# A two-layer hybrid encoder on one core: a table of offsets to the list scheduler's turns

## The chip, the cores and the metric

The kernel runs on one core of a Trainium2 chip. The time is device microseconds (us) of one execution, median of several runs. The profile is one further execution, read with its own time.

## What is computed

Two encoder layers on x (512 tokens, 1024 features, float32). Per layer, shortened from the reference:

```python
h = rmsnorm(x, norm_mix[i])
qa, ka, va, qb, kb, vb, cq, ckv, kr = jnp.split(h @ w_in[i], split_at, axis=-1)
o_a = dilated_attention(rmsnorm(qa), rmsnorm(ka), va, table_a)     # A: 6 heads, whole rows of 512 keys here
o_b = banded_attention(rmsnorm(qb), rmsnorm(kb), vb, 128, bias_b)  # B: 4 heads, +-128 keys, with a sink
o_c = latent_attention(qc, kc, vc)                                 # C: 6 heads, low rank q and kv, rotary part
mixed = concat(rmsnorm(o_a), rmsnorm(o_b), rmsnorm(o_c))
x = x + mixed @ w_out[i]
h = rmsnorm(x, norm_mlp[i])
x = x + square(relu(h @ w_up[i])) @ w_down[i]
```

## The kernel before

Nothing is issued as it is written. `tile_hybrid_encoder_kernel` calls stand-ins of the engines; each call is recorded (`record`, L171) as an `Op` with its number `i` in program order, its modelled cost on each engine that may run it, and the earlier ops that it needs. At the end `schedule` (L207) lists them: at each turn it takes, of all ops whose needs are met and whose buffers can be had, the one that can start first by the model, and of equal ones the one with the lowest number (L251). An op that either ScalarE or VectorE may run (a copy out of PSUM, the high half of a split) goes where `finish` (L225) has it end sooner, and there too the ops with a lower number count as standing ahead. `emit` (L285) then issues the list, so that every engine and the DMA queue of SyncE run in exactly that order and wait by semaphores. All instructions therefore carry line L295.

The work of a layer, in program order: `win0`, `win(1)`, `win(2)` and the steps w3 to w7 (L911) are slices of the input projection; C0 to C2, A0 to A2, B0 and B1 are pairs of heads; `group` normalises a head group; then the output projection over three groups of columns (L928), and the MLP in four chunks (L969). All products are in float32r from a high and a low half (`mm3`, L403): the names `whi` and `wlo` are the halves of a weight tile of 1024 columns, split from `raw`, of which there are two buffers; four of each half are held. `fm` holds halves of activations.

A head (`attend`, L735) goes in halves of two query blocks. For each block TensorE makes scores (`bank<-qk`), VectorE adds the bias and finds the row's extreme (`p<-bank,ma` and `nm`), ScalarE takes the exponential (`p<-p,nm`), TensorE transposes it in four pieces (`bank<-con_sb,p`), ScalarE and VectorE split that into halves (`pt`), and TensorE multiplies by the values (`bank<-pt,v`, for B `bank<-pt,vb`). Between these the only other work for TensorE is projections (`bank<-whi,fm` and `bank<-wlo,fm`).

Queries and keys of A and B must be laid out twice (`pair_t`, L793): from a transposed tile SyncE's queue copies halves of partitions (`qk<-qk`), six for keys, three for queries, some of which wait for others to land. In the same queue stand the weights, the bias rows (`ma<-brow`) and, for the output projection, the tiles of x (`x_tiles`, L341, loaded at L925): three of the four lie in the buffer `v` of A's values, so that their loads cannot start before A's last product has read it. The projection's result is added to x on VectorE (`v<-bank,grc,v`, L936).

Of the kernel before, what the change touches and what calls it, by code (L numbers as in the profile page):

```python
# [2 lines left out]

# [14 lines left out]
D = 1024  # L18
S = 512
# [9 lines left out]

G1, G2, GO, GQL, GKL, GQA, GKA, GQB, GKB, GQC, GKC, GQR, GKR, SNK, NPAR = (  # L30
    0, 8, 16, 24, 26, 27, 28, 29, 30, 31, 32, 33, 65, 97, 101)


def _head(x, n):
# [11 lines left out]
class View:  # L46


    def __init__(self, buf, a, ops, dtype):
        self.buf, self.a, self.ops, self.dtype = buf, a, ops, dtype  # L50
# [65 lines left out]


class Op:
    __slots__ = ("i", "eng", "name", "args", "kw", "alts", "cost", "after", "need", "todo", "at", "bufs", "end", "start")


class Plan:
# [5 lines left out]

    def __init__(self, tc, pools):
        self.tc, self.pools, self.ops, self.order, self.gate = tc, pools, [], {}, None  # L130

    def tile(self, pool, shape, dtype, tag, name, bufs):
        b = Buf(pool, tuple(shape), dtype, tag, name, bufs, pool == "psum")
        self.order.setdefault(tag, []).append(b)
        return b
# [35 lines left out]
    def record(self, eng, method, args, kw, alt=None):  # L171
        out = kw.get("out", args[0] if args else None)
        outs = [v for v in (out, kw.get("accum_out")) if isinstance(v, View)]
        ins = [v for v in list(args) + list(kw.values()) if isinstance(v, View) and all(v is not w for w in outs)]
        cost = self.cost(eng, method, outs[0] if outs else ins[0], ins)
        if kw.get("accum_out") is not None and eng == "scalar":
            cost += 93.0
        if alt:
            alt.alts[eng] = (method, args, kw, cost)
            return  # L180
        o = Op()
        o.i, o.alts = len(self.ops), {eng: (method, args, kw, cost)}
        o.after, o.need, o.bufs = set(), {self.gate} if self.gate else set(), []
        for views, write in ((ins, False), (outs, True)):
            for v in views:
                b, box = v.buf, v.box()
                if b not in o.bufs:
                    o.bufs.append(b)
                    b.left += 1
                keep = []  # L190
                for e in b.log:
                    bx, op, wr = e
                    hit = bx[0] < box[1] and box[0] < bx[1] and bx[2] < box[3] and box[2] < bx[3]
                    if hit and (write or wr) and op is not o:
                        o.need.add(op)
                    inside = box[0] <= bx[0] and bx[1] <= box[1] and box[2] <= bx[2] and bx[3] <= box[3]
                    if not (write and inside and op is not o):
                        keep.append(e)
                keep.append((box, o, write))
                b.log = keep  # L200
        for p in o.need:
            p.after.add(o)
        o.todo, o.at, o.end = len(o.need), 0.0, None
        self.ops.append(o)
        return o

    def schedule(self):  # L207
        self.order = {t: [b for b in bs if b.left] for t, bs in self.order.items()}
        free = {t: [0.0] * bs[0].bufs for t, bs in self.order.items()}
        head = {t: 0 for t in self.order}  # L210
        placed = set()
        ready = {}
        clock = {}
        for o in self.ops:
            for e in o.alts:
                clock[e] = 0.0
                if not o.todo:
                    ready.setdefault(e, []).append(o)
        result = []
        while len(result) < len(self.ops):  # L220
            best = None
            queue = {e: [(o.i, o.alts[e][3]) for o in c if len(o.alts) == 1 and o.at <= clock[e] + 500.0]
                     for e, c in ready.items()}

            def finish(o, e):  # L225

                wait = 0.25 * sum(x for i, x in queue[e] if i < o.i)
                return max(clock[e], o.at) + wait + o.alts[e][3] + self.LATER.get(e, 0.0)

            for e, c in ready.items():  # L230
                for o in c:
                    if len(o.alts) > 1 and min(o.alts, key=lambda x: finish(o, x)) != e:
                        continue
                    at = max(o.at, clock[e])
                    for b in o.bufs:
                        if b in placed:
                            continue
                        f = free[b.tag]
                        seq = self.order[b.tag]
                        while seq and head[b.tag] < len(seq) and seq[head[b.tag]] in placed:  # L240
                            head[b.tag] += 1
                        skip = 0
                        for x in seq[head[b.tag]:] if b.tag not in self.ANY_ORDER else ():
                            if x is b:
                                break
                            skip += x not in placed
                        if skip >= len(f):
                            at = None
                            break
                        at = max(at, sorted(f)[skip])  # L250
                    if at is not None and (best is None or (at, o.i) < best[:2]):  # L251
                        best = (at, o.i, o, e)
            if best is None:
                raise RuntimeError("no instruction can be issued")
            at, _, o, e = best
            o.eng = e
            o.name, o.args, o.kw, o.cost = o.alts[e]
            o.start, o.end = at, at + o.cost
            clock[e] = o.end
            for a in o.alts:  # L260
                ready[a].remove(o)
            for b in o.bufs:
                if b in placed:
                    continue
                f = free[b.tag]
                f.sort()
                f.pop(max(n for n, x in enumerate(f) if x <= at))
                placed.add(b)
            result.append(o)
            lat = self.LAT[e]  # L270
            for b in o.bufs:
                b.left -= 1
                b.end = max(b.end, o.end + lat)
                if not b.left:
                    free[b.tag].append(b.end)
            for d in o.after:
                d.todo -= 1
                to_pe = "tensor" in d.alts
                d.at = max(d.at, o.end + (0.0 if e == "tensor" and to_pe else lat + (130.0 if to_pe else 0.0)))
                if not d.todo:  # L280
                    for a in d.alts:
                        ready.setdefault(a, []).append(d)
        return result
# [871 lines left out]
```

## Time and profile before

| | |
|---|---|
| time, median of 3 runs | 1229.56 us (1227.28 to 1229.75) |
| the profiled execution: its own time | 1230.45 us |
| its span, first to last instruction | 1228.7 us |
| TensorE matmul busy | 1203.5 us, 98%, 6624 instructions |
| TensorE weight loads busy | 1032.6 us, 84% |
| VectorE busy | 1014.5 us, 83% |
| ScalarE busy | 629.0 us, 51% |
| DMA, mean share of 16 engines | 31.7% for the queue of SyncE |
| mean granted TensorE clock | 0.993 |

1.75 us of the profiled time lie around the span. A matmul's record is longer than the interval to the next one, since they overlap in the array; so a busy share of 98% says that TensorE seldom stood quite empty, and not that it was fed as fast as it can go. The interval between starts tells the rate. The granted clock is a share of 2.4 GHz: 1.00 is 2.4 GHz, 0.50 is 1.2 GHz.

### The profile page before, as it was taken

How to read it: one execution, taken by the hardware profiler on the slowest of the kernel's cores; microseconds unless marked ns; L12 is line 12 of the kernel's file. 1: busy time of each engine (PE TensorE's matmuls, PEld its weight loads, DVE VectorE, ACT ScalarE, POOL GpSimd, SP SyncE). 2: the span in 40 equal slices, each digit the busy share in tenths (PEclk: the TensorE clock that was granted, in tenths of full speed). 3: DMA queues.
4: the chain of work that ended last, by engine and by line, in shares of the span. 5: the costliest groups of instructions: out<-in, count | busy, mean ns of one | idle time of the engine just before them, and what ended most of it. 6: DMA issues, size and time to landing. Idle time of an engine off the chain costs nothing.

```text
span 1228.7 us, 17782 instructions
## 1 busy us (share of the span) xinstructions
PE 1203.5 (98%) x6624; PEld 1032.6 (84%) x6624; DVE 1014.5 (83%) x1907; ACT 629.0 (51%) x1232; POOL 3.5 (0%) x10
## 2 busy tenths in 40 slices
PE   9999999899999999999999999898999999999998
PEld 8998979788888888888899989786888888888886
DVE  7799879798796886977958996997978869779686
ACT  6658678455343333333546684965544334334342
POOL 1000000000000000000000000000000000000000
PEclk9999999899999999999999999998999999999999
DMA  6311254533133042140152114454331422422301
GB/s 197 125 52 53 50 147 132 150 137 121 68 122 118 35 173 102 71 135 20 53 166 72 50 52 102 136 146 136 131 117 38 165 79 79 155 71 103 103 1 69
DMA packets 36357, 123.89 MB, mean 101 GB/s; under 512 B 4700, under 2 KB 5852, under 8 KB 32176
## 3 DMA queue, kind: packets, MB, share of 16 engines
q1 hardware_dynamic: 36048, 122.41, 31.7%
q8 instruction: 52, 0.85, 0.3%
q0 software_dynamic: 224, 0.36, 0.1%
q14 instruction: 33, 0.27, 0.1%
HBM read 108.29 MB, written 4.24 MB: 92 GB/s over the span
## 4 chain that ended last, share of the span: by engine, by line
PE 85%; ACT 7%; DVE 4%; DMA 2%; issue 2%; SPq 0%; ACTq 0%; DVEq 0%
PE bank L295 85%; ACT p L295 3%; ACT pt L295 2%; DVE p L295 1%; DVE pt L295 1%; ACT pvt L295 1%; ACT sq L295 1%; DVE wlo L295 1%; DMA v<-in_xT_dram 0%; DMA qk<-qk 0%; DVE v L295 0%; ACT tm L295 0%; DMA v<-in_x_dram 0%; DVE o L295 0%; ACT fm L295 0%
## 5 line engine op out<-in xcount | busy, mean ns | idle before, releaser
L295 PE MATMUL bank<-fm,whi 128*128 128x512 f32 x1024 | 315.8, 390 | 0.0
L295 PE MATMUL bank<-whi,fm 128*128 128x256 f32 (+2 forms) x1280 | 288.2, 310 | 1.3 <-ACT whi L295 1.0
L295 PEld LDWEIGHTS bank<-fm,whi 128*128 128x128 f32 x1024 | 192.2, 188 | 39.9
L295 PEld LDWEIGHTS bank<-whi,fm 128*128 128x128 f32 x1280 | 211.5, 190 | 13.0 <-ACT whi L295 1.3
L295 ACT ACTIVATE whi<-raw 128x1024 fp32r<-128x1024 f32 (+2 forms) x110 | 112.3, 1023 | 209.0 <-PE bank L295 157.1
L295 DVE TENSOR_TENSOR wlo<-raw,whi 128x1024 fp32r<-128x1024 f32 (+2 forms) x122 | 142.4, 1169 | 79.3 <-ACT whi L295 78.9
L295 PE MATMUL bank<-fm,wlo 128*128 128x512 f32 x512 | 199.3, 390 | 0.0
L295 PE MATMUL bank<-wlo,fm 128*128 128x256 f32 (+2 forms) x640 | 197.3, 309 | 0.2 <-DVE wlo L295 0.2
L295 PE MATMUL bank<-whi,tm 128*128 128x512 f32 x544 | 177.2, 390 | 0.0
L295 PEld LDWEIGHTS bank<-wlo,fm 128*128 128x128 f32 x640 | 121.6, 190 | 6.4 <-DVE fm L295 0.9
L295 ACT ACTIVATE whi<-pt 128x1024 fp32r<-128x1024 f32 x64 | 68.0, 1063 | 109.6 <-PE bank L295 90.1
L295 PEld LDWEIGHTS bank<-whi,tm 128*128 128x128 f32 x544 | 102.1, 188 | 22.2
L295 PE MATMUL bank<-wlo,tm 128*128 128x512 f32 x304 | 118.7, 390 | 0.0
L295 PEld LDWEIGHTS bank<-fm,wlo 128*128 128x128 f32 x512 | 96.1, 188 | 19.9
L295 ACT ACTIVATE whi<-qk 128x1024 fp32r<-128x1024 f32 x48 | 50.9, 1059 | 100.7 <-PE bank L295 100.7
L295 PE MATMUL bank<-qk 96*128 96x512 f32 (+3 forms) x304 | 89.8, 401 | 5.6 <-issue 4.5
L295 DVE TENSOR_TENSOR wlo<-qk,whi 128x1024 fp32r<-128x1024 f32 x48 | 57.9, 1219 | 31.0 <-ACT whi L295 31.0
L295 DVE TENSOR_TENSOR pt<-bank,pt 128x512 fp32r<-128x512 f32 (+2 forms) x128 | 79.4, 633 | 4.1 <-ACT pt L295 2.3
L295 PE MATMUL bank<-con_sb,p 128*128 128x128 f32 x464 | 75.9, 285 | 5.8 <-DVE nm L295 1.7
L295 DVE TENSOR_TENSOR wlo<-pt,whi 128x1024 fp32r<-128x1024 f32 x64 | 77.9, 1217 | 1.2 <-ACT whi L295 1.2
L295 ACT ACTIVATE pt<-bank 128x512 fp32r<-128x512 f32 (+2 forms) x128 | 68.7, 555 | 3.3 <-PE bank L295 2.0
L295 ACT ACTIVATE p<-p,nm 128x512 f32<-128x512 f32 (+2 forms) x80 | 52.0, 651 | 33.6 <-DVE nm L295 33.5
(182 smaller groups left out, 1867.6 us busy)
## 6 DMA issues: line engine op xcount, KB each, us to landing
qk<-in_w_down_dram SPq DMA_DIRECT2D x32, 1024.0 KB, 4.6
raw<-in_w_up_dram SPq DMA_DIRECT2D x64, 512.0 KB, 3.3
raw<-in_w_in_dram SPq DMA_DIRECT2D x28, 512.0 KB, 3.4
qk<-qk SPq DMA_DIRECT2D x78, 128.0 KB, 2.4
raw<-in_w_out_dram SPq DMA_DIRECT2D x16, 512.0 KB, 3.8
ma<-brow SPq DMA_DIRECT2D x12, 448.0 KB, 4.0
raw<-in_w_in_dram SPq DMA_DIRECT2D x8, 288.0 KB, 3.6
v<-in_xT_dram SPq DMA_DIRECT2D x6, 256.0 KB, 6.2
```

What stands on the lines that cost most here:

```text
L295: getattr(getattr(nc, o.eng), o.name)(*[real(a) for a in o.args], **{k: real(v) for k, v in o.kw.items()})
```

## The change

The scheduler gets a table of 1220 offsets, one per eight consecutive ops. An op's turn is its number plus its offset (from -4058 to 1332, 312 on average without sign), and turns take the place of numbers in the two comparisons named above. The recorded ops, their costs in the model, and the buffers are the same.

```diff
+TURNS = (
+    'c-qBP`FB>;72W53kqQ(GBEd*d5=6j=U|<EM0?`bBjYxw)0@y+%LZvLU42wAwrPwHzA_^iyFfJiM)Rs~T2&Qp?f@Kg<B&f(F$Rq(0$b0vm-D8$r'
...
+)
@@ class Plan
+        self.turns = np.frombuffer(zlib.decompress(base64.b85decode(TURNS)), "<i2")
@@ record
+        o.turn = o.i + int(self.turns[o.i // 8])
@@ schedule
-            queue = {e: [(o.i, o.alts[e][3]) for o in c if len(o.alts) == 1 and o.at <= clock[e] + 500.0]
+            queue = {e: [(o.turn, o.alts[e][3]) for o in c if len(o.alts) == 1 and o.at <= clock[e] + 500.0]
...
-                wait = 0.25 * sum(x for i, x in queue[e] if i < o.i)
+                wait = 0.25 * sum(x for i, x in queue[e] if i < o.turn)
...
-                    if at is not None and (best is None or (at, o.i) < best[:2]):
-                        best = (at, o.i, o, e)
+                    if at is not None and (best is None or (at, o.turn, o.i) < best[:3]):
+                        best = (at, o.turn, o.i, o, e)
...
-            at, _, o, e = best
+            at, _, _, o, e = best
```

What comes out differs nearly everywhere in the attention stages, in both layers, and in parts of the MLP. Of the 9755 ops, 67 change engine: 31 copies go from ScalarE to VectorE (18 of them high halves of weight tiles) and 36 the other way. All lines stand 31 further down, so that L295 reads L326. Three places follow.

**SyncE's queue at the first layer's output projection.** Before, the three loads of x into `v` stand among the copies of `pair_t`:

```order
L295 DMA qk<-qk 64x512 x4
L295 DMA v<-in_x_dram 128x1024
L295 DMA qk<-qk 64x512 x2
L295 DMA v<-in_x_dram 128x1024
L295 DMA qk<-qk 64x512 x5
L295 DMA v<-in_x_dram 128x1024
L295 DMA qk<-qk 64x512
```

Now:

```order
L326 DMA raw<-in_w_out_dram 128x1024
L326 DMA v<-in_x_dram 128x1024 x2
L326 DMA qk<-qk 64x512
L326 DMA v<-in_x_dram 128x1024
L326 DMA qk<-qk 64x512 x5
```

The third load stood behind eleven copies and now stands behind one, ahead of the run of five. In the second layer (where x comes from `xs`) the order before is as in the first; there it is now:

```order
L326 DMA v<-xs 128x1024
L326 DMA qk<-qk 64x512 x4
L326 DMA v<-xs 128x1024
L326 DMA qk<-qk 64x512 x2
L326 DMA v<-xs 128x1024
L326 DMA qk<-qk 64x512 x5
```

Here the third load stands behind six copies, and ahead of the five.

**TensorE in the A heads of the first layer.** Before, after the last projection matmul of w6 no other follows for 113 matmuls (the same in the second layer); they begin so:

```order
L295 MATMUL bank<-whi,fm 128x256
L295 MATMUL bank<-con_sb,p 128x128 x12
L295 MATMUL bank<-pt,v 128x256
L295 MATMUL bank<-con_sb,p 128x128 x2
L295 MATMUL bank<-pt,v 128x256 x7
L295 MATMUL bank<-con_sb,p 128x128 x5
L295 MATMUL bank<-pt,v 128x256
L295 MATMUL bank<-con_sb,p 128x128
L295 MATMUL bank<-qk 128x512
```

Now, at the same amount of matmul work from the start:

```order
L326 MATMUL bank<-whi,fm 128x256 x2
L326 MATMUL bank<-con_sb,p 128x128 x4
L326 MATMUL bank<-pt,v 128x256 x7
L326 MATMUL bank<-wlo,fm 128x256
L326 MATMUL bank<-whi,fm 128x256 x2
L326 MATMUL bank<-wlo,fm 128x256
L326 MATMUL bank<-whi,fm 128x256
L326 MATMUL bank<-con_sb,p 128x128 x2
L326 MATMUL bank<-pt,v 128x256 x8
```

Projection matmuls now stand between the transposes and the products. The longest stretch of A without one is 33 matmuls in the first layer and 29 in the second.

**TensorE at the start of the B heads of the first layer.** Before:

```order
L295 MATMUL bank<-qk 128x256 x2
L295 MATMUL bank<-wlo,fm 128x512
L295 MATMUL bank<-whi,fm 128x512
L295 MATMUL bank<-qk 128x256 x2
L295 MATMUL bank<-qk 128x384 x4
L295 MATMUL bank<-con_sb,p 128x128 x2
L295 MATMUL bank<-qk 128x256 x2
```

From the fourth row on 75 matmuls follow without a projection. Now:

```order
L326 MATMUL bank<-qk 128x384 x2
L326 MATMUL bank<-whi,fm 128x512 x2
L326 MATMUL bank<-con_sb,p 128x128 x2
L326 MATMUL bank<-wlo,fm 128x512
L326 MATMUL bank<-qk 128x384 x2
L326 MATMUL bank<-whi,fm 128x512
L326 MATMUL bank<-con_sb,p 128x128 x3
L326 MATMUL bank<-qk 128x384 x2
```

From the row with three transposes on, 55 follow without one; in the second layer 75 before and 71 now.

## Rows read from the trace of the kernel before

**Rows 1.** The page: busy time of the engines, share of the span, instructions.

```profile
PE 1203.5 (98%) x6624; PEld 1032.6 (84%) x6624; DVE 1014.5 (83%) x1907; ACT 629.0 (51%) x1232; POOL 3.5 (0%) x10
```

**Rows 2.** Sums over stretches: us, busy PE, PEld, DVE, ACT, POOL, clock, DMA, GB/s.

```profile
307.20:337.90 30.70, 30.70 (x136) 25.30 (x135) 22.67 (x31) 11.55 (x14) 0.00 (x0) 1.00 0.20 68
...
92.00:130.00 38.00, 36.74 (x254) 32.26 (x253) 36.67 (x69) 32.52 (x77) 0.00 (x0) 1.00 0.13 43
...
164.00:188.00 24.00, 21.81 (x152) 18.02 (x151) 22.82 (x58) 23.50 (x61) 0.00 (x0) 1.00 0.42 129
...
230.00:242.00 12.00, 8.60 (x37) 6.61 (x38) 8.41 (x30) 7.76 (x28) 0.00 (x0) 0.72 0.33 119
...
836.00:850.00 14.00, 10.46 (x44) 7.98 (x43) 8.97 (x31) 8.32 (x29) 0.00 (x0) 0.63 0.31 111
```

**Rows 3.** PE in order of time: start, us, engine, line, instruction, count. Dense places.

```profile
93.50 0.28 PE L295 MATMUL bank<-whi,fm 128*128 128x256 f32 x1
93.62 0.40 PE L295 MATMUL bank<-qk 96*128 96x512 f32 x1
...
99.84 0.28 PE L295 MATMUL bank<-whi,fm 128*128 128x256 f32 x1
...
253.11 0.84 PE L295 MATMUL bank<-con_sb,p 128*128 128x128 f32 x6
253.71 0.48 PE L295 MATMUL bank<-whi,fm 128*128 128x512 f32 x1
```

**Rows 4.** The same view: ends of the A heads' run of 113, both layers.

```profile
163.54 1.84 PE L295 MATMUL bank<-con_sb,p 128*128 128x128 f32 x12 [0.76 <-ACT v L295]
...
182.91 0.36 PE L295 MATMUL bank<-whi,fm 128*128 128x256 f32 x1
...
769.92 0.63 PE L295 MATMUL bank<-con_sb,p 128*128 128x128 f32 x4 [0.76 <-ACT v L295]
...
789.28 0.36 PE L295 MATMUL bank<-whi,fm 128*128 128x256 f32 x1
```

**Rows 5.** SyncE's queue in order of time, at the loads of x, both layers.

```profile
223.02 3.59 SPq L295 DMA_DIRECT2D qk<-qk  x5
226.65 0.59 SPq L295 DMA_DIRECT2D v<-in_x_dram  x1
...
829.42 3.83 SPq L295 DMA_DIRECT2D qk<-qk  x5
833.30 0.59 SPq L295 DMA_DIRECT2D v<-xs  x1
```

**Rows 6.** VectorE and PE in order of time, where the B heads begin.

```profile
229.44 0.40 PE L295 MATMUL bank<-whi,fm 128*128 128x512 f32 x1
231.08 1.41 DVE L295 SCALAR_TENSOR_TENSOR v<-bank,grc,v 128x512 f32<-128x512 f32 x2 [3.56 <-DMA v<-in_x_dram]
...
231.93 1.68 PE L295 MATMUL bank<-qk 128*128 128x256 f32 x6 [2.09 <-issue]
...
835.85 0.40 PE L295 MATMUL bank<-whi,fm 128*128 128x512 f32 x1
...
837.80 1.41 DVE L295 SCALAR_TENSOR_TENSOR v<-bank,grc,v 128x512 f32<-128x512 f32 x2 [4.18 <-DMA v<-xs]
...
838.65 2.26 PE L295 MATMUL bank<-qk 128*128 128x256 f32 x6 [2.41 <-issue]
```

**Rows 7.** PE in order of time: the ends of the B heads' run of 75.

```profile
247.94 0.50 PE L295 MATMUL bank<-whi,fm 128*128 128x512 f32 x1
...
855.43 0.50 PE L295 MATMUL bank<-whi,fm 128*128 128x512 f32 x1
```

**Rows 8.** Groups by shape: line engine op names shapes xcount | busy us, mean ns | idle before.

```profile
L295 DVE TENSOR_TENSOR wlo<-raw,whi 128x1024 fp32r<-128x1024 f32 x108 | 131.4, 1219 | 68.8 <-ACT whi L295 68.5
...
L295 ACT ACTIVATE whi<-raw 128x1024 fp32r<-128x1024 f32 x98 | 103.8, 1061 | 194.2 <-PE bank L295 148.7 <-DMA raw<-in_w_up_dram 27.0 <-DMA raw<-in_w_in_dram 18.4
...
L295 DVE CAST whi<-raw 128x1024 fp32r<-128x1024 f32 x10 | 6.9, 686 | 2.2 <-PE bank L295 2.2
```

More of the change, by code (lines that the diff above doesn't have):

```diff
@@ L1 @@
+import base64
 import math
+import zlib
 from contextlib import ExitStack
@@ L31 @@
     0, 8, 16, 24, 26, 27, 28, 29, 30, 31, 32, 33, 65, 97, 101)
+TURNS = (
+    'c-qBP`FB>;72W53kqQ(GBEd*d5=6j=U|<EM0?`bBjYxw)0@y+%LZvLU42wAwrPwHzA_^iyFfJiM)Rs~T2&Qp?f@Kg<B&f(F$Rq(0$b0vm-D8$r'
+    '{S$n9eeZ|w-FMzSdpNg5bKUhmHSFWQmKAzNUDVcJiuPzV`pHU8W0B-=laIqvKT?~@m(nU$2XZmrccY>~Ze`s;7lu{WhSWZI<(=BnuqDe}<f?*~'
+    ';u^#~D3`g^C!n*e(Nl6+%WzD#(&_h6AD8Ol!f9@-wsH%79Ut&RT!Ef+7hD(rf);X)4)<-*PzNZ(Cw*UGa7fx9HAs#%it8yma4W~lVKzf|$&<Zd'
+    'Ro!>B^Q!N-xaacln%6JBer0{Q^XlW*j$U0}J2Twx{t>-%bwk)ax)jw!t+j@mxZkI_v2}B!Sk!<QIT>Yqmu--M7I+#%xQgRc2`DOf!Vl4g+Jpm`'
+    'f{wBoW8^lOB7Jp%jFkuE5Y^}Cx4xMyV=rCnCUHEMv5`LOb9@VyMdRHX|4K9}T<pH)av2b$@@;*U6}*Lu*bB+*jTv0XPH4swf4g3cdbtDsq;=I2'
+    'T`?5*Arm)pGUKHXo?CSR=fGo>+{4poCfhO1kMQL>SCcfC)BPA<>@(32A2AC(@Cs%jNh)|1xl*NHVoMMow<Z`ZtC?%7M=)JZahLUefXWiwj7v!5'
+    'KmdP27WP2UPBM{$HGmXh2lJW6JTFM)T<*oJpiAty{0=WMowq=AHmfz%lRg<KIKpqE1ixO}V=NQ-zTU0J^&@?fSIkHM=BIoF!?1_PwU(XTQI3<N'
+    '7$!61Ik_lP@QrMf^Grjr#LG~L6XkDF!bZFf=XuUp%0e9`%j+^F2;~JS2x?F!TO~cH4T|KZ*u$~pxQ}Cx$G!?4iR*S<`?xpckN77S>1WzWSGiNV'
+    '&$sgxex5%PZHy+mweGmPFIwW>*L#?y7tPr@{x)6bUUP%=6JGKoG~hr+T*>#i)qV*mz$h%Q=XIU#<E<EnH@Qzg)t-1<#&Rl`=mO2+W-dlfa7O;j'
+    'p8BvZVyT|csf_2-e3XNk$NqNjjbGv*%W;%RXoJ?~x`x=!j%bc#)4L0{us<@;4R<1Dop->8{EA16=}Ok|B`mSE7r2K3ZoqES@Oqq9@2Y)cjr<kA'
+    'Qt=aAqxrm6@^*O@<>+X<rSmLeB1qvwTIARICv>KMX+G(M&pFgzcDsBlpX>8Y-A?+lFXNp!i&V?tCZ1t}HpeE}g8qC=-wSrh0htgK%kyp|Q?$~z'
+    '^p9|xUI}N{%?kI0C!#W!9mPjs_?audcG9wz=Sst~VP=%1U3ISx(-v|nEDsN0fh>>Bj!lm>iq%TDU<mSLuuPJhG1yf`C(OUAw4ZOMjkVOD_19~f'
+    'mWLH}`O%6f!=K{|vBV%VRwU0zrjFnstaD$xk<oPX^23~Ec-A`p8#kC9JGq}RtmoS-L{roDR_t@T?2RWa8{N<z8+p<uPFHlm1b)wRuDO)RLKy_F'
+    'PvI?gXA}0~%lx%X$=%w5S(c$}rtme+w2IZdiJ|`7^xwjN@fo(TDkJ!Wzn5M3p^o7VFgKVpnj(QeGxvn-Xa9N2_<kPd-?@U@?5)*I;%V;SeB1R5'
+    'lDm10H<;&VbBw;BhqcN(bN+cwVgn4oCmexW;P`u+D<iR!-{4UkLF2drd=;#h?BEiPp%`0P!}aFUMEiCMmSQ6cnW5t_1HZvtmX!kT)Kbl`c{7aZ'
+    'x`S8E(<Qd<e&iwB)+FFpxWpSJRf_Qz)?y&$VJ1Gui<l!Hi49{M;v5-m)wf$OA8;oAVznQ_6b!fet1UgRnv=YpN;l#*w8cFrK@uKAJ~vpEK5S`;'
+    'OTk{0Vh8r&6&}&Mm`aiFY%&GxYW;uVKlZ&{mfP&|{5vk+=ldc*(5LxipX6HVB%Poe^(NlTgL+o?YX=sZ64jc9yK&e~j7nqYAycCY<BgAbSd8PG'
+    'h@SYsv>eBf1MF!lEaPQnVxnY88+jAm1d=Ep%W|7_%aD)R#$&BC3u3VqHpkY=Ijz&}>}xts#b0gL{n6X1+|MtJjtg91)1#MvO3(Wj^`MsHU7oU&'
+    'qN!|<))F6dwtf8~h#4v*SN<SDkP|!=%n9DG*_18a&9%d9AG3oRnH-D`It4vqPX`r<$A658`PO4S<v-EY(9&@ya*>ET>d_I$c#MZM$6T?*I8LfZ'
+    '^B<qyVQT*mEzPL~C`7s;$0}skqpzK#4a~tm;QwC<>T%FA+1<EGvajs0OjI&Y=d*#*M}BubGBiV1`u%Rc8|({xjn<kfXLO;R;HylDAMm-IS-UMo'
+    'YG`cx>tISZL1(*n=Dmh2_NYfsHZq3e?fFiwwRFA3b@qFXebBFdNB;$F0C$K'
+)
@@ L118 @@
 class Op:
-    __slots__ = ("i", "eng", "name", "args", "kw", "alts", "cost", "after", "need", "todo", "at", "bufs", "end", "start")
+    __slots__ = ("i", "eng", "name", "args", "kw", "alts", "cost", "after", "need", "todo", "at", "bufs", "end", "start", "turn")
 class Plan:
```

## The prediction

> **What bounds the kernel now.** I read the page first. TensorE is busy for 98% of the span [rows 1], so no gap of any size seems left. But a matmul's record overlaps the next one's, and the interval between starts tells more. In a stretch of the MLP 136 matmuls of 512 columns fill 30.70 us [rows 2], 0.226 us each; one of 256 columns starts 0.12 us before the next, and six transposes take from 253.11 to 253.71, 0.10 us each [rows 3]. These are the dense rates. For 384 and 128 columns I take 0.174 and 0.065, estimates in proportion.
>
> Then I asked where the rate is missed. In the MLP it isn't. It is in the attention stages, and there at two places per layer, which the order of TensorE explains: long runs in which no projection matmul stands between the heads' own, so that every round over ScalarE and VectorE is waited out.
>
> *A heads.* The run of 113 matmuls lasts from 163.54 to 182.91, 19.37 us [rows 4]. It holds 56 transposes, 41 products of 256 columns and 16 scores of 512: 56 x 0.10 + 41 x 0.12 + 16 x 0.226 = 14.1 us. So 5.2 us are lost. In the second layer it lasts from 769.92 to 789.28 [rows 4], the same 5.2 us. The waits listed are below 1 us each; the rest is spread over short intervals that the view doesn't list as idle.
>
> *Entry to the B heads.* The third load of x is issued at 226.65, after five copies that hold SyncE's queue for 3.59 us [rows 5]. VectorE has come to the addition that needs it and stands for 3.56 us, until 231.08, 4.4 us after the issue [rows 6]. Behind it in VectorE's order stand additions that free PSUM banks, and TensorE, out of other work, stands idle 2.09 us until 231.93 [rows 6]. What follows is the run of 75 without cover, until 247.94 [rows 7], and in it the granted clock falls: 0.72 over 230 to 242 [rows 2], that is, part of it at 1.2 GHz instead of 2.4. From the end of the last projection matmul (start 229.44, 0.23 later 229.67 [rows 6]) to 247.94 it is 18.3 us. The 75 are 29 transposes, 26 of 256 columns, 12 of 384 and 8 of 128: 2.9 + 3.1 + 2.1 + 0.5 = 8.6 us. Lost: 9.7 us. The second layer has the same picture: queue held 3.83 us [rows 5], VectorE 4.18 and TensorE 2.41 us idle [rows 6], clock 0.63 over 836 to 850 [rows 2]; from 836.08 to 855.43 [rows 6, 7] 19.35 us, lost 10.7 us.
>
> Together the four places lose 5.2 + 5.2 + 9.7 + 10.7 = 30.8 us. That is what an order alone can win here.
>
> **The change, part by part.**
>
> *The load of x.* In the first layer the third load now stands ahead of the five copies and behind one only; in the second behind six, ahead of the five. So the 3.59 and 3.83 us in the queue [rows 5] go from before it. In the first layer its load then begins nearly as soon as the values' buffer is free, and between that and its use there is more VectorE work than the 4.4 us that a load takes; I cost that wait at nothing. In the second layer VectorE has only about 4 us of work ahead of its first addition of x, against 4.4 to 4.5 us from issue to use [rows 5, 6]. I put 1.2 us there, between nothing and the 2.41 us that TensorE stood [rows 6]. What covers both is the output projection's matmuls; if they ran out, the old 2.09 us [rows 6] would be back.
>
> *The B run.* It shrinks from 75 to 55 and to 71 matmuls. It still waits for its own rounds. Its price at full clock I take from the A run, 5.2 us for 113, or 0.046 each: 55 x 0.046 = 2.5 us and 71 x 0.046 = 3.3 us. The idle entry and the fall of the clock go, as I read it, with the stall that precedes them. Saved: 9.7 - 2.5 = 7.2 and 10.7 - 3.3 - 1.2 = 6.2, together 13.4 us. Bounds: nothing (all of it is the B heads' own latency), and 20.4 us (all gone).
>
> *The A run.* It breaks up into stretches of at most 33 and 29, with projections between. What a short one loses: the run of 39 in C lasts from 93.62 to 99.84 [rows 3], 6.2 us, and holds 16 transposes, 8 of 256 and 15 of 512 columns, 5.9 us; so 0.3 us. Several of these come in a layer; I leave 1.5 us per layer, and save 3.7 + 3.7 = 7.4 us. Bounds: nothing, since VectorE is at 22.82 of 24 us there [rows 2], and 10.4.
>
> *The C heads.* Their longest run falls from 146 matmuls to 48 in the first layer, 38 in the second. VectorE is busy for 36.67 of 38 us in that stretch [rows 2], and the work there is unchanged: I count nothing, between nothing and about 2 us per layer.
>
> *The MLP.* Here the change can only cost, since nothing is lost now. Before, splits of weights run well ahead of use. Counted in the order with its waits, some 80 places now wait for work on the other engines that could begin only 5 to 15 matmuls before, where there were 7 such places. A high half takes 1.061 us on ScalarE or 0.686 on VectorE, the low half 1.219 more [rows 8]; seven matmuls are 1.58 us, five 1.13, ten 2.26. So lead and work are about equal, nearly covered. I take 0.06 us each, 5 us in all: bounds nothing, and 0.25 each (a whole interval of a matmul), 20 us.
>
> *The 67 copies that change engine* go with this: 18 high halves on VectorE are 18 x 0.686 = 12 us of its time, mostly in the MLP, where it has 8 of 30.7 us free [rows 2]: nothing on the path.
>
> **The sum.** 1230.45 (the profiled execution's own time) - 13.4 - 7.4 + 5 = 1214.7. The median of the runs shown is 0.9 us lower than the profiled execution, so 1213.8; I say 1214.
>
> **Rivals.**
>
> 1. *Only the A part comes.* B stays as it is, because its price is its own latency and the clock falls there in any case. For it: 71 of 75 matmuls in the second layer still stand without cover. Against it: the clock is at 1.00 through the A run and through the C heads [rows 2], which wait on the same rounds. Saved 7.4, and 5 given back: 1227. With half of B's 13.4 it is 1220.5. The Trainium skill ("TensorE: Matmul & The Clock Gate", Part 4: PE-mode transpose) says that transposes don't count as activity for the clock gate in the way matmuls do; by that, a run with 29 transposes in 75 could lose the clock without any stall, and 1220 to 1227 would be the result. The trace speaks against it so far: 92 to 130, with C's runs of transposes, shows 1.00 [rows 2].
>
> 2. *VectorE is the bound.* It is at 95 to 97% over the A and C heads [rows 2]. If so, projections between the heads only move the waiting to where they are missing later, and the time stays near 1229. Against it: it has room elsewhere in the stage, 8.41 of 12 us busy at the entry to B [rows 2].
>
> 3. *Slower: the MLP's splits come too late.* One mechanism: at a weight buffer's turn VectorE has another instruction of 1.219 us [rows 8] in front, and the low half misses its matmul. With 80 places, this decides from 20.8 / 80 = 0.26 us per place. If 0.7 us is missed at half of them, that is 28 us: 1230.45 - 20.8 + 28 - 0.9 = 1236.8. For it: leads are about equal to the work. Against it: in the MLP ScalarE is busy 11.55 and VectorE 22.67 of 30.70 us [rows 2], so a long row of instructions in front should be rare.
>
> **How the numbers follow.** The forecast has a chance of 0.6, with its own range from 1206 to 1220. Rival 1 has 0.2 (1220 to 1227). Rival 2 has 0.09, rival 3 has 0.11. Changes below 0.2%, 2.5 us, can't be told from none here. So faster is 0.6 + 0.2 = 0.80, the same 0.09, slower 0.11. The range from 1204 to 1228 takes in the forecast with the upper part of both savings (another 9 us), and rival 1; it leaves out the other two, 0.2.
>
> **What would show it.** Right: the third load of x in the first layer is issued before the five copies, and VectorE's wait for it is below 1 us; TensorE's idle of 2.09 us at the entry to B is gone, and the granted clock stays at 1.00 there; the A heads' stretch has projections among the transposes and no wait over 0.5 us. The MLP shows waits of TensorE for `whi` and `wlo` of less than 5 us in sum. Wrong: the clock at 0.5 somewhere in B (rival 1); the same time for the attention stage with VectorE at 95% or more throughout (rival 2); an MLP chunk that is longer by more than 2 us (rival 3).

## The result, and the profile after

The changed kernel takes 1210.81 us (median of 4 runs, 1210.50 to 1211.73), the kernel before beside it 1228.42 us (4 runs): a ratio of 0.9858, 95% interval 0.9843 to 0.9872. That is 17.6 us less, against a forecast of 1214.

The page of the profiled execution after (its own time 1210.97 us, span 1209.0): busy time of the engines, and the chain that ended last, by engine. They answer to [rows 1].

```profile
PE 1194.9 (99%) x6624; PEld 1028.3 (85%) x6624; DVE 1008.5 (83%) x1902; ACT 638.9 (53%) x1237; POOL 3.5 (0%) x10
...
PE 89%; ACT 4%; DVE 3%; DMA 1%; issue 1%; SPq 0%; ACTq 0%; DVEq 0%
```

The same line of the chain before:

```profile
PE 85%; ACT 7%; DVE 4%; DMA 2%; issue 2%; SPq 0%; ACTq 0%; DVEq 0%
```

The instructions and VectorE's work are nearly as before; what is gone is time between matmuls. To see where, I took the start of all 6624 matmuls from both traces and set side by side those before which the same amount of TensorE's work is done, counted at the dense rates (0.227 us for 512 columns, 0.12 for 256, 0.107 for a transpose, and so on).

| stretch, bounded by matmuls | before, us | after, us | difference |
|---|---|---|---|
| start of the program | 71.56 | 71.98 | +0.4 |
| C heads, first layer | 90.85 | 90.46 | -0.4 |
| A heads, first layer | 62.65 | 58.38 | -4.3 |
| output projection's entry and B heads, first layer | 65.77 | 60.45 | -5.3 |
| MLP, first layer | 390.65 | 390.77 | +0.1 |
| projection and C heads, second layer | 88.44 | 87.90 | -0.5 |
| A heads, second layer | 57.45 | 53.92 | -3.5 |
| entry and B heads, second layer | 87.06 | 81.43 | -5.6 |
| MLP, second layer | 309.15 | 309.47 | +0.3 |
| sum, to the start of the last matmul | 1223.58 | 1204.76 | -18.8 |

So A gives 7.8 us, B 10.9, C 0.9, and the MLP and the start take 0.4 each. C's 0.4 us in the first layer is no effect of the change: by the same count that stretch is 0.4 us shorter, too, in the kernels of experiments 1 (the load early) and 3 (B alone), whose C heads run as before. (The two profiled executions differ by 19.5 us; the rest lies after the last matmul.)

**The load of x.** SyncE's queue in order of time, at the third load of each layer; it answers to [rows 5].

```profile
217.68 0.58 SPq L326 DMA_DIRECT2D v<-in_x_dram  x1
218.31 6.36 SPq L326 DMA_DIRECT2D qk<-qk  x5
...
818.10 0.58 SPq L326 DMA_DIRECT2D v<-xs  x1
821.46 3.30 SPq L326 DMA_DIRECT2D qk<-qk  x5
```

In both layers the third load goes out ahead of the five copies. VectorE's waits show none for a load of x, where there were 3.56 and 4.18 us [rows 6].

**The entry to B.** VectorE and PE in order of time; it answers to [rows 6, 7].

```profile
224.33 0.48 DVE L326 CUSTOM_DVE_ANT_0 p<-bank,ma,nsk 128x256 f32<-128x256 f32 x1
...
226.61 0.40 PE L326 MATMUL bank<-whi,fm 128*128 128x512 f32 x1
...
232.46 0.52 PE L326 MATMUL bank<-con_sb,p 128*128 128x128 f32 x3 [0.79 <-DVE nm L326]
...
236.98 0.50 PE L326 MATMUL bank<-whi,fm 128*128 128x512 f32 x1
...
828.56 0.48 DVE L326 CUSTOM_DVE_ANT_0 p<-bank,ma,nsk 128x256 f32<-128x256 f32 x1
...
832.18 0.40 PE L326 MATMUL bank<-whi,fm 128*128 128x512 f32 x1
832.98 0.92 PE L326 MATMUL bank<-con_sb,p 128*128 128x128 f32 x6 [0.41 <-DVE pt L326]
...
844.91 0.50 PE L326 MATMUL bank<-whi,fm 128*128 128x512 f32 x1 [0.24 <-DVE o L326]
```

The first softmax step in the kernel before, both layers:

```profile
232.44 0.48 DVE L295 CUSTOM_DVE_ANT_0 p<-bank,ma,nsk 128x256 f32<-128x256 f32 x1
...
839.26 0.48 DVE L295 CUSTOM_DVE_ANT_0 p<-bank,ma,nsk 128x256 f32<-128x256 f32 x1
```

The first softmax step of B (`p<-bank,ma`) now starts at 224.33, 2.5 us ahead of the end of the last projection matmul (226.61 + 0.23); in the second layer at 828.56, 3.85 us ahead. Before, it came after the stall, at 232.44 and 839.26, 2.8 and 3.2 us behind that end. The run without a projection lasts from 226.84 to 236.98, 10.1 us for 55 matmuls that are 6.2 us at the dense rates, so 3.9 us are lost; in the second layer from 832.41 to 844.91, 12.5 us for 7.9, so 4.6. No wait is above 0.8 us.

Sums over stretches of these runs, of the A heads and of the MLP; the columns are those of [rows 2], the clock is the third figure from the right.

```profile
226.00:237.00 11.00, 9.46 (x62) 7.37 (x60) 10.16 (x41) 10.85 (x40) 0.00 (x0) 1.00 0.41 133
...
825.00:840.00 15.00, 14.09 (x80) 11.12 (x79) 14.51 (x47) 10.32 (x35) 0.00 (x0) 1.00 0.72 223
...
156.00:181.00 25.00, 24.52 (x188) 22.85 (x188) 22.90 (x64) 21.73 (x57) 0.00 (x0) 1.00 0.65 167
...
300.00:330.70 30.70, 30.70 (x136) 25.23 (x136) 27.18 (x36) 13.80 (x17) 0.00 (x0) 1.00 0.20 69
```

The granted clock is 1.00 through both B runs, where it was 0.72 and 0.63 [rows 2]. In the A heads TensorE is busy for 24.52 of 25 us, where it was 21.81 of 24, and VectorE is no busier (92% against 95%). In the MLP 136 matmuls fill 30.70 us, as before.

**A heads.** PE in order of time, first layer; it answers to [rows 4].

```profile
162.19 0.41 PE L326 MATMUL bank<-whi,fm 128*128 128x256 f32 x2
162.44 0.60 PE L326 MATMUL bank<-con_sb,p 128*128 128x128 f32 x4
162.80 1.07 PE L326 MATMUL bank<-pt,v 128*128 128x256 f32 x7
163.70 0.28 PE L326 MATMUL bank<-wlo,fm 128*128 128x256 f32 x1
163.82 0.40 PE L326 MATMUL bank<-whi,fm 128*128 128x256 f32 x2
```

Transposes, products and projections follow each other at the dense intervals: seven products from 162.80 to 163.70, with a projection at once behind them. The longest wait listed for PE in this stretch (156 to 181) is 0.48 us, once, for a copy of keys.

### The profile page after: what moved, and what is told of

Read it like the earlier page. It is cut to its first block, busy times and chain, and to the rows that moved or that the text cites. A ratio compares the mean times of both kernels' runs of the same rounds, so it can differ in the third digit from the quotient of the medians.

```text
span 1209.0 us, 17753 instructions
## 1 busy us (share of the span) xinstructions
PE 1194.9 (99%) x6624; PEld 1028.3 (85%) x6624; DVE 1008.5 (83%) x1902; ACT 638.9 (53%) x1237; POOL 3.5 (0%) x10
## 4 chain that ended last, share of the span: by engine, by line
PE 89%; ACT 4%; DVE 3%; DMA 1%; issue 1%; SPq 0%; ACTq 0%; DVEq 0%
PE bank L326 89%; ACT p L326 1%; ACT pt L326 1%; DMA qk<-qk 1%; ACT sq L326 0%; DMA v<-in_xT_dram 0%; DVE v L326 0%; ACT pvt L326 0%; DVE pt L326 0%; DVE qk L326 0%; DMA raw<-in_w_out_dram 0%; DVE o L326 0%; DVE p L326 0%; ACT tm L326 0%; DVE tm L326 0%
## 5 line engine op out<-in xcount | busy, mean ns | idle before, releaser
L326 PE MATMUL bank<-fm,whi 128*128 128x512 f32 x1024 | 315.0, 390 | 0.0
L326 PE MATMUL bank<-whi,fm 128*128 128x256 f32 (+2 forms) x1280 | 289.9, 311 | 1.7 <-ACT fm L326 0.8
L326 PEld LDWEIGHTS bank<-fm,whi 128*128 128x128 f32 x1024 | 192.1, 188 | 40.3
L326 PEld LDWEIGHTS bank<-whi,fm 128*128 128x128 f32 x1280 | 211.7, 190 | 13.6 <-ACT whi L326 1.0
L326 PE MATMUL bank<-wlo,fm 128*128 128x256 f32 (+2 forms) x640 | 196.4, 310 | 0.0
L326 PE MATMUL bank<-fm,wlo 128*128 128x512 f32 x512 | 196.3, 390 | 0.0
L326 ACT ACTIVATE whi<-raw 128x1024 fp32r<-128x1024 f32 (+2 forms) x102 | 105.0, 1032 | 168.5 <-PE bank L326 125.0
L326 DVE TENSOR_TENSOR wlo<-raw,whi 128x1024 fp32r<-128x1024 f32 (+2 forms) x122 | 142.2, 1170 | 60.1 <-ACT whi L326 59.5
L326 PE MATMUL bank<-whi,tm 128*128 128x512 f32 x544 | 178.4, 391 | 0.0
L326 PEld LDWEIGHTS bank<-wlo,fm 128*128 128x128 f32 x640 | 121.2, 190 | 5.3 <-DVE wlo L326 0.2
L326 ACT ACTIVATE whi<-pt 128x1024 fp32r<-128x1024 f32 x61 | 64.4, 1061 | 113.4 <-PE bank L326 80.3
L326 PEld LDWEIGHTS bank<-whi,tm 128*128 128x128 f32 x544 | 102.1, 188 | 22.4
L326 PE MATMUL bank<-wlo,tm 128*128 128x512 f32 x304 | 118.1, 391 | 0.0
L326 PEld LDWEIGHTS bank<-fm,wlo 128*128 128x128 f32 x512 | 96.1, 188 | 20.2
L326 PE MATMUL bank<-qk 96*128 96x512 f32 (+3 forms) x304 | 89.1, 395 | 1.4 <-DMA qk<-qk 0.5
L326 DVE TENSOR_TENSOR pt<-bank,pt 128x512 fp32r<-128x512 f32 (+2 forms) x128 | 79.5, 634 | 5.4 <-ACT pt L326 4.3
L326 DVE TENSOR_TENSOR wlo<-pt,whi 128x1024 fp32r<-128x1024 f32 x64 | 77.6, 1218 | 5.8 <-ACT whi L326 5.6
L326 ACT ACTIVATE whi<-qk 128x1024 fp32r<-128x1024 f32 x45 | 47.5, 1059 | 59.8 <-PE bank L326 59.8
L326 PE MATMUL bank<-con_sb,p 128*128 128x128 f32 x464 | 72.9, 275 | 2.8 <-DVE nm L326 1.0
L326 DVE TENSOR_TENSOR wlo<-qk,whi 128x1024 fp32r<-128x1024 f32 x48 | 58.3, 1219 | 19.4 <-ACT whi L326 19.4
L326 ACT ACTIVATE pt<-bank 128x512 fp32r<-128x512 f32 (+2 forms) x125 | 67.0, 552 | 2.3 <-PE bank L326 1.4
L326 PEld LDWEIGHTS bank<-wlo,tm 128*128 128x128 f32 x304 | 57.1, 188 | 12.7 <-DVE wlo L326 0.2
```

The source lines that it names most:

```text
L326: getattr(getattr(nc, o.eng), o.name)(*[real(a) for a in o.args], **{k: real(v) for k, v in o.kw.items()})
```

## The experiments

The kernel before ran again beside them, at 1228.56 (experiments 1 and 4) and 1228.61 us (2, 3 and 5); the changed kernel did not, so differences from it are taken from its 1210.81.

**1. The load alone, in both directions.** In the order before, the third load of x is issued right behind the second; nothing else moves.

```diff
+    for i, behind in ((2647, 2646), (7507, 7506)):
+        result.remove(at[i])
+        result.insert(result.index(at[behind]) + 1, at[i])
```

> Theory 1 (the stall of VectorE at the third load of x makes TensorE stand, and the granted clock falls with that): VectorE's 3.56 and 4.18 us and TensorE's 2.09 and 2.41 us are gone, the clock is 1.00 through both runs of 75 matmuls, and each run loses 75 x 0.046 = 3.5 us instead of 9.7 and 10.7: about 13.4 us less, 1215 us. Theory 2 (75 matmuls without cover lose the clock by themselves): only TensorE's two waits go, 4.5 us, 1224 us, and the clock still falls. Theory 3 (the stall moves to the next wait): 1228 us.

1224.81 us, a ratio of 0.9971 (0.9960 to 0.9982): 3.75 us less, the number of theory 2 (its falling clock shows in the first layer alone). The first layer, VectorE and PE in order of time:

```profile
227.83 1.43 PE L303 MATMUL bank<-qk 128*128 128x256 f32 x8 [1.17 <-DVE v L303]
...
230.47 0.75 DVE L303 SCALAR_TENSOR_TENSOR v<-bank,grc,v 128x512 f32<-128x512 f32 x1 [2.81 <-PE bank L303]
231.13 0.48 DVE L303 CUSTOM_DVE_ANT_0 p<-bank,ma,nsk 128x256 f32<-128x256 f32 x1
```

VectorE's waits for loads of x are 0.6 us in sum now; but then it waits 2.81 us for the last projection, which its order has ahead of the first softmax step. So the softmax starts at 231.13, 0.9 us after the end of the last projection (230.03 + 0.23), and the run of 75 is as uncovered as it was. The clock, in this run:

```profile
236.00:242.00 6.00, 5.97 (x34) 5.08 (x33) 4.74 (x16) 5.08 (x18) 0.00 (x0) 0.76 0.43 160
...
834.00:842.00 8.00, 5.70 (x33) 3.96 (x31) 5.57 (x22) 5.39 (x20) 0.00 (x0) 1.00 0.38 125
```

It still falls in the first layer, less than before, and not in the second. From the last projection's end, the runs of 75 lose 7.3 and 6.6 us with the early load, against 9.7 and 10.7 before. The second one, PE in order of time:

```profile
835.07 0.39 PE L303 MATMUL bank<-qk 128*128 128x256 f32 x2
...
850.34 0.50 PE L303 MATMUL bank<-whi,fm 128*128 128x512 f32 x1
```

This run is at 1.00 to its end, and it lasts 15.27 us for 8.6 at the dense rates. In the kernel before the same matmuls in the same order took 16.78 us from the first one on (838.65 to 855.43 [rows 6, 7]), some 10 us of it at 1.2 GHz (0.63 over 14 us [rows 2]). So of the 10.7 us lost there, 2.6 are the stall, about 1.5 go with the fall of the clock, and 6.6 are the B heads' own at full clock: 0.088 us for each of the 75.

The other direction: in the order after, the third load goes behind the copies (and the addition that reads it behind the load).

```diff
+    for i, behind in ((2647, 2495), (2687, 2647), (7507, 7222), (7547, 7507)):
```

> Theory 1: the stall is back in both layers, VectorE stands over 3 us at the third load, TensorE about 2 us, and the clock falls below 1.00 in the B heads: 5 us per layer, 1221 us. Theory 2 (it is the cover by projections that counts, not the load): below 2 us in all, 1211 to 1213 us, clock 1.00 in both layers. By the run lengths the second layer, with 71 matmuls, should then be the worse one.

1218.32 us (1215.39 to 1222.74, 6 runs), 7.5 us more than after. The queue, VectorE and PE in the second layer:

```profile
821.81 8.53 SPq L334 DMA_DIRECT2D qk<-qk  x7
830.38 0.59 SPq L334 DMA_DIRECT2D v<-xs  x1
...
834.07 0.75 DVE L334 SCALAR_TENSOR_TENSOR v<-bank,grc,v 128x512 f32<-128x512 f32 x1 [3.28 <-DMA v<-xs]
...
834.88 0.80 PE L334 MATMUL bank<-qk 128*128 128x256 f32 x2 [3.36 <-DVE v L334]
```

The stall is back: TensorE stands for 3.36 us (1.99 in the first layer), and the granted clock falls in both layers:

```profile
236.00:242.00 6.00, 5.11 (x28) 4.84 (x28) 4.58 (x17) 3.77 (x13) 0.00 (x0) 0.72 0.12 46
...
834.00:842.00 8.00, 7.12 (x22) 5.89 (x22) 4.96 (x12) 1.74 (x4) 0.00 (x0) 0.57 0.39 115
```

TensorE's order is that of the kernel after, so the two traces can be set side by side matmul by matmul. The profiled execution here (1222.74 us, the slowest) falls behind by 2.0 and 3.4 us at the stalls, by 1.8 us in waits that follow the first one, by 1.2 and 2.7 us while the clock is down, and by 0.6 us at the start of the program: 11.8 us in all, of which the stalls are 5.4 and the clock 3.9. The six executions go with that in the main: 1215.39 us at a mean clock of 1.000, 1216.41 at 0.999, 1216.74 at 0.997, 1220.45 at 0.995, 1222.74 at 0.994, but also 1219.91 at 0.999, which neither explains. The load is needed for B's gain, but by itself, in the order before, it brings only a third of it.

**2. Cover at the entry to B.** In the order after, for the second layer alone, everything of B between its first score and the last projection is issued behind those projections. No load moves.

```diff
+    a, b = number.index(7294), number.index(7655) + 1
+    late = [o for o in result[a:b] if 7203 <= o.i < 7483 and o.eng != "sync"]
+    result[a:b] = [o for o in result[a:b] if o not in late] + late
```

> The order after, but in the second layer's entry to B the projections are issued ahead of all of B's work that they stood among; loads unmoved. Now the first softmax of B starts 3.85 us ahead of the end of the last projection. Theory 1 (this lead is what covers the first round): it goes, 3.9 us more, 1214.7 us. Theory 2 (the early load is enough): 1211 us. Theory 3 (the length of the run decides, 87 matmuls instead of 71 at 0.046 each): 0.7 us more, 1211.5 us.

1213.33 us (1212.05 to 1215.53), 2.5 us more than after. PE and VectorE in order of time:

```profile
829.38 0.39 PE L334 MATMUL bank<-whi,fm 128*128 128x512 f32 x1
...
831.68 0.48 DVE L334 CUSTOM_DVE_ANT_0 p<-bank,ma,nsk 128x256 f32<-128x256 f32 x1
...
847.11 0.50 PE L334 MATMUL bank<-whi,fm 128*128 128x512 f32 x1 [0.24 <-DVE o L334]
```

The first softmax starts at 831.68, 2.1 us behind the end of the last projection instead of 3.85 ahead; the run of 87 lasts 17.5 us for 10.2 at the dense rates and loses 7.3 us, not 4.6. So the early load is not enough, and the length of the run at 0.046 is too small. Theory 1 has the sign, but of a lead that fell by 5.9 us less than half is paid. The edit also lengthens the run: 16 more matmuls at the 0.065 us that the run of 71 loses for each (4.6 / 71) would be 1.0 of the 2.5 us, so how much the lead alone is worth is not shown. The clock stayed at 1.00 here.

**3. Offsets of some stages alone.** The table is set to zero elsewhere.

```diff
+        n = np.arange(len(self.turns))
+        self.turns[~((n >= 0) & (n < 293) | (n >= 619) & (n < 900))] = 0
```

> Offsets up to the end of the A stage only. Theory 1 (the gain in A belongs to A's order): 4.4 and 3.3 us from A and 1.6 from C, 9.3 us, come; the B heads keep their loss in the first layer, where five copies again stand ahead of the third load of x, and lose 3.3 us less in the second, where the order has the load ahead of the copies by itself: 1216 us. Theory 2 (what A wins is waited for at B): above 1222 us.

1217.82 us (1216.60 to 1219.56; ratio 0.9918, 0.9900 to 0.9936): theory 1, 2 us off. A's gain is there by itself: by the same count as in the table above, the stretch of its run loses 1.2 and 0.7 us instead of 4.8 in each layer, and the two stretches of A are 4.1 and 3.1 us shorter than before. What theory 1 did not have is the split at B: with B's own offsets at zero the stretches of the entry and B are 3.3 and 1.9 us shorter, so about half of B's 10.9 us comes with what stands ahead of it. In the first layer five copies stand ahead of the third load, but it is issued at 220.16, when VectorE does not need it yet, and there is no stall.

> Offsets of the B heads and the output projection only. The order has 76 uncovered matmuls with the load late in the first layer, and 86 with all three loads early in the second. Theory 1 (load and cover are both needed): the first layer is unchanged, the second wins the 3.3 us of the earlier run with the load moved: 1225 us. Theory 2 (B's offsets bring B's gain by themselves): 1217 us.

(Kept here: 293 to 370 and 900 to 978.) 1236.59 us, slower than before (1.0064, 1.0049 to 1.0079); neither theory. The first layer's run of 76, with the load late (VectorE stands 3.0 us for it), lasts from 228.83 to 249.99, 21.2 us for 8.6; the second's of 86 from 846.05 to 868.23, 22.2 us for 9.7. In the second all three loads go out together ahead of the copies, nothing waits for them, and it loses 12.4 us all the same. Sums of these two kernels, of the one with C and A first:

```profile
834.00:842.00 8.00, 6.55 (x28) 5.70 (x29) 6.17 (x26) 6.54 (x24) 0.00 (x0) 0.58 0.73 242
```

and of the one with B alone:

```profile
236.00:242.00 6.00, 5.04 (x20) 3.58 (x18) 3.43 (x14) 4.70 (x18) 0.00 (x0) 0.50 0.67 238
...
850.00:858.00 8.00, 6.26 (x27) 4.86 (x27) 5.49 (x22) 6.56 (x24) 0.00 (x0) 0.76 0.66 221
```

In the second layer of both the clock falls with no load late. B's offsets cost 8.0 us by themselves; behind those of C and A they win (experiment 4).

**4. The MLP.** Its offsets zeroed (kept: 0 to 370, 619 to 978), and the reverse.

> Theory 1 (the leads of the weight splits in the MLP are enough, its new order costs nothing): 1210.8 us within 1. Theory 2 (the MLP's new order costs the 5 us that the prediction put there, and the attention stages win 5 more than they seem to): 1206 us. Theory 3 (the MLP's new order wins something): above 1212 us.

1213.46 us (1212.96 to 1214.66), 2.65 us more than after: the MLP's offsets win a little, at the second layer's entry to its first chunk, where by the count of the table about 2 us are lost instead of 0.1. Theory 3, and the opposite of the prediction's sign. The kernel before loses 0.2 us at that place, so these offsets mend what the new order ahead would cost there; they speed up nothing that was slow before. With experiment 3 this gives the change stage by stage: the offsets of C and A bring 1228.6 to 1217.8, 10.8 us, B's on top of them 4.4 more (to 1213.5), the MLP's the last 2.7.

> Theory 1 (the MLP's new order costs and wins nothing): 1228.4 us within 1.5. Theory 2 (it costs 5 us): 1233 us. Theory 3 (it wins something): below 1226 us.

1239.28 us (1.0091, 1.0078 to 1.0104): 10.7 us more than before, twice theory 2. The loss sits in the first layer's MLP (11.5 us by the count of the table), most of it in one place. VectorE, ScalarE and PE there, in order of time, and sums over the stretch from 427.4 on:

```profile
417.85 1.23 DVE L328 TENSOR_TENSOR wlo<-qk,whi 128x1024 fp32r<-128x1024 f32 x1 [2.48 <-ACT whi L328]
422.04 1.23 DVE L328 TENSOR_TENSOR wlo<-pt,whi 128x1024 fp32r<-128x1024 f32 x1 [2.97 <-ACT whi L328]
...
424.98 2.35 DVE L328 TENSOR_TENSOR tm<-p,tm 128x1024 fp32r<-128x1024 f32 x2
427.25 1.28 DVE L328 SCALAR_TENSOR_TENSOR p<-bank,sq 128x512 f32<-128x512 f32 x2
...
428.56 0.84 ACT L328 ACTIVATE o<-p 128x768 fp32r<-128x768 f32 x1 [3.74 <-DVE p L328]
...
429.46 0.80 PE L328 MATMUL bank<-whi,o 128*128 128x512 f32 x1 [5.75 <-ACT o L328]
...
427.40:434.30 6.90, 4.84 (x12) 3.80 (x12) 6.05 (x9) 1.86 (x2) 0.00 (x0) 0.51 0.23 71
```

TensorE stands 5.75 us for the hidden half `o`. Its `p<-bank,sq` starts on VectorE at 427.25, though ScalarE had finished `sq` by 414.6: ahead of it VectorE's order has weight splits for later matmuls, for which it stood 2.48 and 2.97 us, and low halves of other hidden tiles. Behind the wait the granted clock is 0.51 over 6.9 us, and there another 2.3 us are lost. So VectorE's order can hold TensorE up in the MLP, as rival 3 feared, but it comes as one large wait by splits that stand too early, not as many small ones by splits that come too late. (Whether moving that one instruction would give the time back wasn't tried.)

**5. One of the two comparisons.** Turns in the tie, op numbers in the choice of engine.

```diff
-            queue = {e: [(o.turn, o.alts[e][3]) for o in c if len(o.alts) == 1 and o.at <= clock[e] + 500.0]
+            queue = {e: [(o.i, o.alts[e][3]) for o in c if len(o.alts) == 1 and o.at <= clock[e] + 500.0]
...
-                wait = 0.25 * sum(x for i, x in queue[e] if i < o.turn)
+                wait = 0.25 * sum(x for i, x in queue[e] if i < o.i)
```

> Turns in the tie between ops only, op numbers again in the choice between ScalarE and VectorE. The order differs much from both: 610 matmuls in runs of 28 and more without a projection, where before has 809 and after 400. Theory 1 (the sum of uncovered matmuls sets the loss, 56.4 us before and 37.5 after, so 0.046 us each): 47 us of loss, 1220.5 us. Theory 2 (it depends on the single places, one stall more or less): off by over 5 us from that.

1249.84 us (1.0171, 1.0155 to 1.0188), 29 us above theory 1. So the sum of uncovered matmuls doesn't set the time. In its second layer the third load is again behind five copies, and the clock is 0.54 over 850 to 858; TensorE's waits, over the whole program, are many (7.5 us for `pt`, 6.3 for `nm`).

No run beats the changed kernel.

## Why the prediction was right

- *What bounds it: TensorE's missed rate in four places.* Right. A and B give 18.7 of the 18.8 us before the last matmul.
- *The A run.* Forecast 7.4 us, found 7.8, and experiment 3 shows it to belong to the order up to A, without that of B.
- *The B run.* Forecast 13.4, found 10.9. The term for what stays was too small: 0.046 us per matmul, taken from the A run. It is 3.9 us for 55 and 4.6 for 71, 0.071 and 0.065 each, with the clock at 1.00, and 0.088 in the run of 75 of experiment 1. So 8.5 us stay where 7.0 were counted; the other 1.0 us is lost outside the two runs. A price per uncovered matmul does not carry from one stage to the next; why B's is higher wasn't tried.
- *"The idle entry and the fall of the clock go with the stall that precedes them."* This step holds only in part. Without the stall, the clock fell in the first layer of experiment 1 and in the second of both kernels of experiment 3. And the fall is a small term: about 1.5 us of the 10.7 in the second layer. The prediction put all that B loses there beyond A's price, some 7 us, to the idle entry and the fall; with the stall's 2.6 us they are 4.1. The load gives 3.75 us by itself. The rest of B's gain goes with B's rounds starting under the projections, 2.5 and 3.85 us ahead of their end, and with shorter runs; experiment 2 shows their sign and not the share of each. The prediction named the projections only as cover for the wait.
- *The load of x in the second layer,* 1.2 us: found nothing; VectorE does not wait for it, and the 0.41 us for which TensorE stands there are for `pt`.
- *C,* nothing: found 0.9 us less, 0.4 of it not from the change.
- *The MLP,* +5 us from 80 places at 0.06 each: found +0.4 in the stretches, and by experiment 4 a gain where the second MLP begins. TensorE's waits for `whi` are 0.5 us in sum, in one place. This was the term that was most wrong. That the sum comes so near is partly luck: the MLP, put 4.6 us too dear, makes up for B, whose saving was put 2.5 us too high. -13.4 - 7.4 + 5 is -15.8, found -18.8; with the MLP at +0.4 the forecast would have been -20.4.
- *Rivals.* Rival 1 has a true part, the clock's fall without a stall, but A's order together with B's avoids it. The Trainium skill ("TensorE: Matmul & The Clock Gate", Part 4: PE-mode transpose) says that a transpose doesn't count as busy for the clock gate in the way a matmul does. The runs here don't single that out: the number of transposes doesn't tell whether a run loses the clock. With 29, both runs before lose it, and so does the first of experiment 1, but not its second, nor the changed kernel's second run; with 31 that of experiment 2 keeps it; with 32 the first run of one kernel of experiment 3 keeps it (C and A) and that of the other loses it (B); with 34 the second runs of both lose it. Rival 2 is refuted by the A stretch: the same VectorE share, more TensorE work. Rival 3 did not occur in the changed kernel.

## What to carry to other kernels

A wait that heads a stall is worth removing, but price what stands behind it: with the load early, VectorE waited 2.81 and 2.60 us for the last projection instead of 3.56 and 4.18 for the load. Before a stage that waits for its own rounds over other engines, look at when its first round starts against the end of the last independent matmul, and at how many matmuls stand without cover after it; here these two changed together with the gain. Offsets in a list scheduler are not separable: parts of this table cost 8 and 11 us where the whole wins 18, so a table is to be measured whole. (That it must be made anew when the code ahead of it changes is likely by this, but no run shows it.)

## What the runs showed of the hardware that was not expected

The same kernel can keep or lose the clock from one execution to the next, and the time goes with it in part. The order after with the load late took 1215.39 us at a mean clock of 1.000 and 1222.74 at 0.994; experiment 2 took 1212.05 to 1213.54 at 1.000 and 1215.53 at 0.997; the kernel before 1230.62 at 0.993 and 1226.00 at 0.996, but also 1226.29 and 1228.20, both at 0.997. The fall also comes where nothing was changed. TensorE's order is the same in the order after with the load late (first row) and in the changed kernel (second row), and near the start of the program the first had a fall and the second had none:

```profile
18.00:26.00 8.00, 8.00 (x43) 6.29 (x42) 7.49 (x24) 2.70 (x4) 0.52 (x1) 0.79 0.44 139
...
18.00:26.00 8.00, 8.00 (x56) 6.29 (x55) 7.23 (x24) 2.84 (x3) 0.52 (x1) 1.00 0.45 137
```

What decides it stays open.

What a fall costs depends on what TensorE has to do. In the second layer's run of 75, where it waits for other engines anyway, some 10 us at 1.2 GHz cost about 1.5 us (experiment 1). Among projections, in the order after with the load late, the 0.57 over 8 us, some 7 us at 1.2 GHz, cost 2.7.
